# Preparing the second chunk's operands in a hybrid decoder layer: two steps per twelve matmuls, loads one piece ahead

## The chip, the cores and the metric

The kernel runs on one core of a Trainium2 chip. The metric is the device time of one execution in microseconds (us), lower is better. Besides the engines TensorE (PE), VectorE (DVE), ScalarE (ACT) and GpSimd (POOL) there is SyncE (SP), whose queue issues all of this kernel's DMAs. Each engine runs its own instructions in the order in which they stand in its queue; semaphores hold an instruction back until what it needs is there.

## The reference

One decoder layer on 2048 tokens of width 1024 in float32. What matters here is its first part: a norm, and one wide projection `w_in`, whose columns are split into attention inputs, a short gated convolution and two gates.

```
xn = rms_norm(h, mix_norm[l])
proj = jnp.einsum("bsd,dp->bsp", xn, w_in[l]) + b_in[l]
q, k, v, cb, cc, cx, ga, gc = jnp.split(proj, splits, axis=-1)
attn = sliding_window_attention(q, k, v, sinks[l])
conv = cb * causal_depthwise_conv(cc * cx, conv_w[l])
merged = (jax.nn.sigmoid(ga) * jnp.einsum("bsc,cd->bsd", attn, w_attn_branch[l])
          + jax.nn.sigmoid(gc) * jnp.einsum("bsc,cd->bsd", conv, w_conv_branch[l]))
h = h + jnp.einsum("bsd,de->bse", merged, w_out[l])
```

After it come a second norm, an up projection with a convolution and a gate, a down projection and a last norm.

## The kernel before

The tokens are cut into four blocks of 512, and two blocks make a chunk. Float32 products are made of three matmuls each: every operand is held as a high and a low half (`split`, L263: ACT casts the high half, DVE subtracts to get the low one).

The input projection (`project_pairs`) runs once per chunk: a first pass over chunk 0 and a second over chunk 1. It takes the 128-column tiles of the weights in pairs, and computes the two tiles of a pair for the two blocks of a chunk with seven half-size products in place of eight (`strassen`, Strassen-Winograd form). Each of the seven is a call of `mms` with twelve matmuls, and these work on prepared combinations: four weight tiles per pair, called A, S21, S3 and S4, and seven operands of the tokens, x1_0 to x1_6 for the second chunk. The weights of a pair come as two raw loads, `wra` (L194) and `wrb` (L195), and are combined and split on DVE and ACT into `wh` tiles (L264, L265); A comes from `wra` alone. A `wh` tile is fetched three uses ahead.

The first pass has fourteen pairs, numbered 3 to 16: six of the convolution's inputs (3 to 8), then eight of gates (9 to 16). For pair f the order is A (two products), S4 of the pair before (two), S21 (two), S3 (one). Between products ACT copies partial sums out of PSUM: at L818 after A's first product, at L827 after S21's first, at L833 after S3's, at L809 after S4's last. The copy at L827 has one product, the other one of S21, before PE needs its bank again. For gate pairs ACT then computes the sigmoid (L494) and SP stores it (`sgd`, L496). For convolution pairs the function `take` uses two `a` buffers, and the results `cvh`, `cvl` are stored at L516 and L517.

Beside the first pass the second chunk is prepared, by a generator named `fill`. `mms` calls `next(fill)` once after its twelve matmuls, and each call records one step. The steps are: `norm1` for blocks 2 and 3 (two rounds of loads L354 and L363, and a store `xnd` L347), and then `x_operands(1)`. That makes eight pieces, one for each of four row tiles and two halves of 256 tokens. A piece is one run of `operands`: four loads `xb` (L746), a sum on DVE (L749), two more on DVE (L752, L754), four casts `xoh` on ACT and four subtractions `xol` on DVE, and fourteen stores `xopd` (L741, L742) of the seven operands, high and low. It has five steps, the first of which is the loads, and its tiles are all from the pool `e`, which has seven buffers of 128x512 and is also used by S3's weight sums and the convolution's results. The second pass loads the stored operands (L782) as x1.

A scheduler orders the recorded instructions of each engine before the program is built. So the queue's order differs from the order of the code by some rows.

Of the kernel before, what the change touches and what calls it, by code (L numbers as in the profile page):

```python
# [21 lines left out]
F32 = mybir.dt.float32  # L22
# [5 lines left out]
P = 128  # L28
S = 2048
D = 1024  # L30
T = 512
# [65 lines left out]
def layer_kernel(ctx: ExitStack, tc: tile.TileContext, x, w, bcol, g1, g2, gf, cw, fcw, sinks, out):  # L97
# [9 lines left out]
    pool = {"wr": p_wr}  # L107
# [8 lines left out]
    def dram(name, shape, dt=F32):  # L116
        return p_d.tile(shape, dt, name=name, tag=name)
# [7 lines left out]
    xn_d = [[dram(f"xnd{c}_{k}", [P, T]) for k in range(KD)] for c in range(NCH)]  # L125
    xop_d = [[dram(f"xopd{d}_{i}", [P, 2, 4, T]) for i in range(7)] for d in range(2)]
# [18 lines left out]
    state = {"next": 0, "use": 0}  # L145
# [138 lines left out]
    def row_tile(name, tag, bufs=1):  # L284
        return p_rows.tile([P, T], F32, name=name, tag=tag, bufs=bufs)
# [63 lines left out]
    def norm1(c):  # L349

        acc = row_tile(f"acca{c}", "acc")
        for k in range(KD):
            t = tmp(f"xs{c}_{k}")
            nc.sync.dma_start(out=t, in_=x[c, k])  # L354
            square_sum(acc, t, k)
            yield
        rows = {}
        rstd_later(acc, f"a{c}", lambda rb: rows.update(rb=rb))
        while not rows:
            yield  # L360
        for k in range(KD):
            t = tmp(f"xn{c}_{k}")
            nc.sync.dma_start(out=t, in_=x[c, k])  # L363
            scale_x(c, k, t, rows["rb"])
            yield

    def x_operands(d):
        for k in range(4):
            for h in range(2):
                yield from operands(d, k, "x", xn_d, xop_d[d], slice(h * T // 2, (h + 1) * T // 2), "e", "e")  # L370

    def take_k(c, src):
        hi, lo = (tmp(f"k{s}{c}", dt=F32R) for s in "hl")
# [101 lines left out]
    def project_pairs(d, xs, fill, early):  # L475
        ccs, ys = {}, {}

        def begin(f, n, u):
            i = PAIRS[f][n]
            if I_CX <= i < I_GA:  # L480
                if d == 0:
                    nc.gpsimd.memset(u[:, 0:2], 0.0)
                else:
                    nc.scalar.copy(out=u[:, 0:2], in_=uh[:, i - I_CX, :])

        def done(f, g, v):
            for n, t in enumerate((g, v)):
                take(PAIRS[f][n], t, t[:, 2:])

        def take(i, t, whole):  # L490
            halves = [(2 * d + n, whole[:, n * T:(n + 1) * T]) for n in range(2)]
            b = bc[:, i:i + 1]
            if i >= I_GA:
                nc.scalar.activation(out=whole, in_=whole, func=AF.Sigmoid, bias=b)  # L494
                for c, half in halves:
                    nc.sync.dma_start(out=sg_d[c][(i - I_GA) % 8][:, (i - I_GA) // 8, :], in_=half)  # L496
            elif i >= I_CX:
                ct = i - I_CX
                nc.vector.scalar_tensor_tensor(out=whole, in0=whole, scalar=b, in1=ccs.pop(ct), op0=ALU.add, op1=ALU.mult)
                nc.scalar.copy(out=uh[:, ct, :], in_=t[:, 2 * T:])  # L500
                ys[ct] = y = pool["a"].tile([P, 2 * T], F32, name=f"cy{d}_{ct}", tag="a")
                nc.scalar.activation(out=y, in_=whole, func=AF.Copy, scale=cwc[:, ct * 3 + 2:ct * 3 + 3])
                for k in (1, 0):
                    nc.vector.scalar_tensor_tensor(out=y, in0=t[:, k:k + 2 * T], scalar=cwc[:, ct * 3 + k:ct * 3 + k + 1],
                                                   in1=y, op0=ALU.mult, op1=ALU.add)
            elif i >= I_CC:
                ccs[i - I_CC] = cc = pool["a"].tile([P, 2 * T], F32, name=f"cc{d}_{i}", tag="a")
                nc.scalar.activation(out=cc, in_=whole, func=AF.Identity, bias=b)
            elif i >= I_CB:
                ct = i - I_CB  # L510
                y = ys.pop(ct)
                nc.vector.scalar_tensor_tensor(out=y, in0=whole, scalar=b, in1=y, op0=ALU.add, op1=ALU.mult)
                for n, (c, _) in enumerate(halves):
                    hi, lo = (tmp(f"cv{s}{c}_{ct}", dt=F32R) for s in "hl")
                    split(hi, lo, y[:, n * T:(n + 1) * T])
                    nc.sync.dma_start(out=conv_d[c][:, 0, ct, :], in_=hi.bitcast(F32))  # L516
                    nc.sync.dma_start(out=conv_d[c][:, 1, ct, :], in_=lo.bitcast(F32))  # L517
            else:
                for c, half in halves:
                    if i == I_K:  # L520
                        take_k(c, half)
                    elif i == I_V:
                        take_v(c, half)
                    else:
                        take_q(c, i - I_Q, half)

        xs.extend(load_x(xop_d[d], f"x{d}", i) for i in range(len(xs), 5))
        return strassen(d, FIRST[d], xs, lambda: [load_x(xop_d[d], f"x{d}", i) for i in range(len(xs), 7)], begin, done,
                        early, fill)
# [188 lines left out]
    def operands(d, k, name, src, dst, cs, big, split_to, direct={}):  # L718

        n_cs = cs.stop - cs.start

        def get(what, tag, dt=F32):
            return pool[tag].tile([P, 2, n_cs], dt, name=f"{name}{what}{d}_{k}_{cs.start}", tag=tag)

        def out(src, places):

            here = [i for i, place in enumerate(places) if place in direct]  # L730
            for i in here:
                if places[i] < 2:
                    continue
                split(*(direct[places[i]][:, s, k, cs] for s in range(2)), src[:, i, :])
            n = len(here)
            if n == len(places):
                return
            hi, lo = (get(f"o{s}{places[0]}_", split_to, F32R)[:, n:len(places), :] for s in "hl")
            split(hi, lo, src[:, n:, :])
            for i, place in enumerate(places[n:]):  # L740
                nc.sync.dma_start(out=dst[place][:, 0, k, cs], in_=hi[:, i, :].bitcast(F32))  # L741
                nc.sync.dma_start(out=dst[place][:, 1, k, cs], in_=lo[:, i, :].bitcast(F32))  # L742

        b1, b2 = get("b1_", big), get("b2_", big)
        for t, i, n, kk in ((b1, 0, 0, k), (b1, 1, 1, k + 4), (b2, 0, 1, k), (b2, 1, 0, k + 4)):
            nc.sync.dma_start(out=t[:, i, :], in_=src[2 * d + n][kk][:, cs])  # L746
        yield
        t13 = get("t_", big)
        nc.vector.tensor_tensor(out=t13, in0=b1, in1=b2[:, 0:1, :].to_broadcast([P, 2, n_cs]), op=ALU.subtract)  # L749
        out(b2[:, 1:2, :], [1])  # L750
        yield
        nc.vector.scalar_tensor_tensor(out=b2[:, 0, :], in0=b1[:, 1, :], scalar=-1.0, in1=t13[:, 0, :], op0=ALU.mult,  # L752
                                       op1=ALU.subtract)
        nc.vector.scalar_tensor_tensor(out=b2[:, 1, :], in0=b2[:, 0, :], scalar=-1.0, in1=b2[:, 1, :], op0=ALU.mult,  # L754
                                       op1=ALU.subtract)
        out(b1, [0, 5])
        yield
        out(t13, [3, 4])
        yield
        out(b2, [2, 6])  # L760
        yield
# [190 lines left out]
    with ExitStack() as inp:  # L952
        def ipool(name, bufs):
            return inp.enter_context(tc.tile_pool(name=f"{name}i", bufs=bufs))

        pool.update(a=ipool("a", 2), wrf=ipool("wrf", 3), e=ipool("e", 7), u=ipool("u", 3), x7=ipool("x7", 1))
        bc = load_const(bcol, [P, 34], "bc")
        xs = plain()
        g2c = load_const(g2, [P, KD], "g2c")
        gfc = load_const(gf, [P, KD], "gfc")  # L960
        cwc = load_const(cw, [P, 12], "cwc")
        fcwc = load_const(fcw, [P, 3 * 2 * NF], "fcwc")
        sinkb = load_const(sinks.to_broadcast([P, NH]), [P, NH], "sinkb")
        fill = chain(norm1(2), norm1(3), x_operands(1))
        xs = project_pairs(0, xs, fill, lambda: [load_x(xop_d[1], "x1", i) for i in range(2)])
        for _ in fill:
            pass
        early = project_pairs(1, xs, iter(()), lambda: [load_t16(q_d[0], "q0"), load_t16(conv_d[0], "conv0")])
        for what in ("x7", "wrf", "e", "u", "a"):
            del pool[what]  # L970
    with ExitStack() as mix:
# [22 lines left out]
        fill = up_operands(0, "b4", "b4", dict(enumerate(xs)))  # L994
# [79 lines left out]
```

## Time and profile before

| | us |
|---|---|
| median of 3 runs | 2537.17 (2535.75 to 2542.23) |
| profiled execution | 2534.93 |
| its span, first to last instruction | 2533.2 |
| PE busy in the span | 2465.8 |
| first pass of the projection, first to last product in PE's timeline | 78 to 340 |
| loads of pieces (L746), first and last | 211.1 to 313.2 |

The rows shown further on are from one profiled execution. A row of a timeline has the start in us from the span's start, the duration, the engine, the line, the operation, what it writes and reads, and how many were merged; in brackets stands idle time before it and what ended it. SPq is SP's queue of DMA issues: the duration there is that of the issue, not of the transfer. A row of the view of waits says which engine and line waited for which, in us in total, how often, and the longest. A row of the groups has the count, then busy us and the mean in ns, then idle time before it.

### The profile page before, as it was taken

The numbers are of one execution on the slowest core, as the hardware profiler recorded it, in microseconds if no ns is written. First come the engines' busy times: TensorE is split into PE (matmuls) and PEld (weight loads), VectorE is DVE, ScalarE is ACT, GpSimd is POOL, SyncE is SP. The second block draws the span as 40 slices with busy tenths as digits, with TensorE's granted clock in tenths as the row PEclk, the third lists the DMA queues.
The fourth block names the chain that finished last, engine by engine and source line by source line (L and its number), as shares of the span: only waits on it lengthen the run. The fifth ranks groups of instructions, "written<-read, shape, count | busy, mean of one in ns | idle before, by whom it ended". The sixth has DMA issues, their size and how long they took to land.

```text
span 2533.2 us, 30315 instructions
## 1 busy us (share of the span) xinstructions
PE 2465.8 (97%) x11032; PEld 2025.7 (80%) x11032; DVE 1782.6 (70%) x2282; ACT 1119.4 (44%) x1843; POOL 22.6 (1%) x72
## 2 busy tenths in 40 slices
PE   8999999999989898988999999999999999999998
PEld 7888778888868787876888888888888888888886
DVE  8877656664388676776888888755479888875335
ACT  6545444444476353533555555322135555551001
POOL 0000000000000000000000000000000000000000
PEclk9999999999999999999999999999999999999999
DMA  6557895223568869588452333888463333356421
GB/s 197 177 177 238 270 365 174 92 100 112 199 229 283 297 222 322 205 295 313 172 174 101 115 118 100 326 311 304 168 228 116 117 109 100 117 191 256 176 84 67
DMA packets 191221, 488.66 MB, mean 193 GB/s; under 512 B 22112, under 2 KB 41696, under 8 KB 181728
## 3 DMA queue, kind: packets, MB, share of 16 engines
q1 hardware_dynamic: 191072, 486.73, 55.1%
q8 instruction: 86, 1.41, 0.2%
q14 instruction: 63, 0.52, 0.1%
HBM read 325.17 MB, written 161.48 MB: 192 GB/s over the span
## 4 chain that ended last, share of the span: by engine, by line
PE 85%; DMA 6%; DVE 3%; ACT 3%; issue 2%; SPq 2%; POOLq 0%; POOL 0%; DVEq 0%; ACTq 0%
PE upx L795 10%; PE upx L796 10%; PE upx L797 10%; PE dn L248 6%; PE dn L247 6%; PE dn L249 6%; PE upz L797 5%; PE upz L795 5%; PE upz L796 5%; PE upy L797 2%; PE upy L796 2%; PE upy L795 2%; PE wo L247 2%; PE wo L248 2%; PE wo L249 2%
## 5 line engine op out<-in xcount | busy, mean ns | idle before, releaser
L795 PE MATMUL upx<-upx,wh 128*128 128x512 f32 x704 | 277.4, 394 | 5.5 <-ACT u L818 3.9
L796 PE MATMUL upx<-upx,wh 128*128 128x512 f32 x704 | 276.5, 393 | 0.0
L797 PE MATMUL upx<-upx,wh 128*128 128x512 f32 x704 | 276.1, 392 | 0.1
L247 PE MATMUL dn<-act,wh 128*128 128x512 f32 x704 | 274.2, 390 | 0.0
L249 PE MATMUL dn<-act,wh 128*128 128x512 f32 x704 | 274.0, 389 | 0.0
L248 PE MATMUL dn<-act,wh 128*128 128x512 f32 x704 | 273.9, 389 | 0.0
L898 DVE TENSOR_TENSOR hr<-dn,hr 128x512 f32<-128x512 f32 x192 | 131.4, 689 | 198.7 <-PE dn L249 198.6
L856 DVE SCALAR_TENSOR_TENSOR a<-u,fcwc,a 128x1024 f32<-128x1024 f32 x176 | 224.0, 1282 | 50.2 <-ACT a L854 47.5
L264 ACT CAST wh<-ws 128x1024 fp32r<-128x1024 f32 (+1 forms) x150 | 124.8, 834 | 147.5 <-DVE ws L207 68.2
L264 ACT CAST wh<-wr 128x1024 fp32r<-128x1024 f32 (+1 forms) x72 | 69.8, 976 | 258.8 <-PE dn L249 218.8
L795 PE MATMUL upx<-x,wh 128*128 128x512 f32 x440 | 173.1, 393 | 6.6 <-ACT u L827 3.7
L265 DVE TENSOR_TENSOR wh<-ws,wh 128x1024 fp32r<-128x1024 f32 (+1 forms) x150 | 143.1, 955 | 46.7 <-ACT wh L264 46.2
L796 PE MATMUL upx<-x,wh 128*128 128x512 f32 x440 | 172.2, 391 | 0.0
L797 PE MATMUL upx<-x,wh 128*128 128x512 f32 x440 | 172.1, 391 | 0.1
L795 PEld LDWEIGHTS upx<-upx,wh 128*128 128x128 f32 x704 | 132.7, 188 | 36.8 <-ACT u L818 4.3
L797 PEld LDWEIGHTS upx<-upx,wh 128*128 128x128 f32 x704 | 132.7, 189 | 29.9 <-DVE wh L265 0.7
L796 PEld LDWEIGHTS upx<-upx,wh 128*128 128x128 f32 x704 | 132.8, 189 | 28.5
L247 PEld LDWEIGHTS dn<-act,wh 128*128 128x128 f32 x704 | 132.1, 188 | 27.5
L249 PEld LDWEIGHTS dn<-act,wh 128*128 128x128 f32 x704 | 132.1, 188 | 27.5
L248 PEld LDWEIGHTS dn<-act,wh 128*128 128x128 f32 x704 | 132.2, 188 | 27.3
L796 PE MATMUL upz<-upx,wh 128*128 128x512 f32 x352 | 137.1, 389 | 0.8 <-DVE upx L265 0.8
L795 PE MATMUL upz<-upx,wh 128*128 128x512 f32 x352 | 137.1, 389 | 0.0
(274 smaller groups left out, 5385.4 us busy)
## 6 DMA issues: line engine op xcount, KB each, us to landing
act<-actd SPq DMA_DIRECT2D x20, 2048.0 KB, 9.7
wrb<-in_w_dram SPq DMA_DIRECT2D x75, 512.0 KB, 3.7
wra<-in_w_dram SPq DMA_DIRECT2D x75, 512.0 KB, 3.7
wr<-in_w_dram SPq DMA_DIRECT2D x64, 512.0 KB, 5.6
actd<-ach SPq DMA_DIRECT2D x88, 256.0 KB, 2.2
actd<-acl SPq DMA_DIRECT2D x88, 256.0 KB, 2.4
upx<-upd SPq DMA_DIRECT2D x10, 2048.0 KB, 9.4
sgd<-u SPq DMA_DIRECT2D x64, 256.0 KB, 2.9
```

Source lines behind the costliest of these rows:

```text
L247: nc.tensor.matmul(ps, ah, bh, start=start, stop=False)
L248: nc.tensor.matmul(ps, ah, bl, start=False, stop=False)
L249: nc.tensor.matmul(ps, al, bh, start=False, stop=stop)
L264: nc.scalar.copy(out=dh, in_=src)
L265: nc.vector.tensor_sub(out=dl, in0=src, in1=dh.bitcast(F32))
L795: nc.tensor.matmul(bank, ah, bh, start=start and k == 0, stop=False, skip_group_check=True)
L796: nc.tensor.matmul(bank, ah, bl, start=False, stop=False, skip_group_check=True)
L797: nc.tensor.matmul(bank, al, bh, start=False, stop=stop and k == 3, skip_group_check=True)
L856: nc.vector.scalar_tensor_tensor(out=a, in0=u[:, k:k + 2 * T], scalar=w3[k], in1=a, op0=ALU.mult, op1=ALU.add)
L898: nc.vector.tensor_tensor(out=hs[n][j], in0=ps, in1=hs[n][j], op=ALU.add)
```

## The change

Three things are changed. The generator `fill` is wrapped in `twice`, so that a call of `next(fill)` takes two steps. `x_operands` waits with its first piece until the last convolution pair is done (a flag set in `take`), and then records the loads of a piece before the steps of the piece ahead of it. And a piece's four loads go into one tile of the pool `a` (two buffers of 128x1024) in place of two tiles of the pool `e`; its sum `xt` stays in `e`.

```
     def x_operands(d):
-        for k in range(4):
-            for h in range(2):
-                yield from operands(d, k, "x", xn_d, xop_d[d], slice(h * T // 2, (h + 1) * T // 2), "e", "e")
+
+        while not state.get("convolved"):
+            yield
+        parts = [operands(d, k, "x", xn_d, xop_d[d], slice(h * T // 2, (h + 1) * T // 2), "a", "e")
+                 for k in range(4) for h in range(2)]
+        next(parts[0])
+        for n, part in enumerate(parts):
+            if n + 1 < len(parts):
+                next(parts[n + 1])
+            yield from part
+
+    def twice(steps):
+        while True:
+            for _ in range(2):
+                if next(steps, steps) is steps:
+                    return
+            yield
...
+                if ct == 3:
+                    state["convolved"] = True
...
-        b1, b2 = get("b1_", big), get("b2_", big)
+        if big == "a":
+            b = pool["a"].tile([P, 4, n_cs], F32, name=f"{name}b{d}_{k}_{cs.start}", tag="a")
+            b1, b2, big = b[:, :2, :], b[:, 2:, :], split_to
+        else:
+            b1, b2 = get("b1_", big), get("b2_", big)
...
-        fill = chain(norm1(2), norm1(3), x_operands(1))
+        fill = twice(chain(norm1(2), norm1(3), x_operands(1)))
```

The first pass has 98 products. The flag is set after the 44th. Before, the pieces' 40 steps took 40 products; now a piece's four steps after its loads take two products, and the eight pieces sixteen.

The instructions are the same ones, in another order within the first pass; from the second pass on each engine's order is the same as before. The first place is SP's queue, around the raw weights of pair 12 (`wra_12`), the tenth pair of the pass. In the name `xb_1_0_0` the numbers are chunk, row tile and first token of the half; the changed kernel's `xb_0_0` has only the last two. Before, they stood here, right behind the first piece's loads:

```order
L516 DMA convd_141<-cvh_3_1994 128x512
L517 DMA convd_141<-cvl_3_1995 128x512
L363 DMA xn_7_2015<-in_x_dram 128x512
L746 DMA xb_1_0_0_2032<-xnd_0_94 128x256
L746 DMA xb_1_0_0_2032<-xnd_4_106 128x256
L746 DMA xb_1_0_0_2033<-xnd_0_102 128x256
L746 DMA xb_1_0_0_2033<-xnd_4_98 128x256
L347 DMA xnd_7_109<-xn_7_2015 128x512
L741 DMA xopd_1_118<-xoh_1_0_0_2059 128x256
L742 DMA xopd_1_118<-xol_1_0_0_2060 128x256
L741 DMA xopd_0_117<-xoh_1_0_0_2091 128x256
L741 DMA xopd_5_122<-xoh_1_0_0_2091 128x256
```

The next row is `wra_12`. In the changed kernel SP's queue begins the pieces like this (L766 is what was L746, L757 and L758 what were L741 and L742):

```order
L530 DMA convd_140<-cvh_3_1992 128x512
L766 DMA xb_0_0_2019<-xnd_0_94 128x256
L531 DMA convd_140<-cvl_3_1993 128x512
L530 DMA convd_141<-cvh_3_1998 128x512
L531 DMA convd_141<-cvl_3_1999 128x512
L766 DMA xb_0_0_2019<-xnd_4_106 128x256
L766 DMA xb_0_0_2019<-xnd_0_102 128x256
L766 DMA xb_0_0_2019<-xnd_4_98 128x256
```

and comes to the same weights here, behind the stores of the sixth piece (`1_2_256`):

```order
L757 DMA xopd_4_121<-xoh_1_2_256_2435 128x256
L758 DMA xopd_4_121<-xol_1_2_256_2436 128x256
L757 DMA xopd_2_119<-xoh_1_2_256_2443 128x256
L758 DMA xopd_2_119<-xol_1_2_256_2444 128x256
L757 DMA xopd_6_123<-xoh_1_2_256_2443 128x256
L758 DMA xopd_6_123<-xol_1_2_256_2444 128x256
L194 DMA wra_12_2453<-in_w_dram 128x1024
L195 DMA wrb_12_2454<-in_w_dram 128x1024
L766 DMA xb_3_256_2471<-xnd_3_97 128x256
```

From the first `xb` row to `wra_12` it was 9 rows, and now it is 120: 28 loads and 84 stores of pieces, four gate stores, three convolution stores and `wrb_11`. The raw weights of pair 13 follow 38 rows after `wra_12`.

The second place is ACT's queue, from the copy at L827 of pair 11 on. Before:

```order
L827 COPY u_0_11_2252<-upx_11_2249 128x512
L264 CAST xoh_1_1_0_2341<-xb_1_1_0_2292 128x512
L264 CAST xoh_1_1_0_2371<-xt_1_0_2318 128x512
L264 CAST wh_2401<-ws_12_2402 128x1024
L264 CAST xoh_1_1_0_2392<-xb_1_1_0_2293 128x512
L833 ACTIVATE u_0_11_2400<-upx_11_2249 128x512
L818 COPY u_0_12_2430<-upx_12_2427 128x512
```

The cast of `wra_12` stood earlier than these rows. In the changed kernel (L847 is what was L827) it stands among them:

```order
L847 COPY u_0_11_2380<-upx_11_2377 128x512
L264 CAST xoh_1_2_256_2414<-xb_2_256_2317 128x512
L264 CAST xoh_1_2_256_2435<-xt_2_256_2404 128x512
L264 CAST xoh_1_2_256_2443<-xb_2_256_2317 128x512
L264 CAST xoh_1_3_0_2478<-xb_3_0_2399 128x256
L264 CAST xoh_1_3_0_2486<-xb_3_0_2399 128x512
L264 CAST xoh_1_3_0_2507<-xt_3_0_2476 128x512
L264 CAST xoh_1_3_0_2515<-xb_3_0_2399 128x512
L264 CAST wh_2452<-wra_12_2453 128x1024
L264 CAST wh_2530<-wrb_11_2197 128x1024
L264 CAST wh_2593<-ws_12_2594 128x1024
```

Seven casts of the sixth and seventh piece have moved ahead of the cast of `wra_12`.

## The prediction

> **What bounds the kernel now.** I read the page first (spans, busy shares), then who PE waited for in the stretch that the change touches, then the timelines of PE, SP, ACT and DVE around each of those waits. The page's head says that TensorE is the bound:
>
> ```profile
> span 2533.2 us, 30315 instructions
> PE 2465.8 (97%) x11032; PEld 2025.7 (80%) x11032; DVE 1782.6 (70%) x2282; ACT 1119.4 (44%) x1843; POOL 22.6 (1%) x72
> ```
>
> So an edit that leaves the matmuls alone can only move the gaps between them. The view of waits, for PE alone and 60 to 700 us (both passes of the input projection), has all the gaps that the edit can reach:
>
> ```profile
> PE upx L795 <- ACT u L827: 3.7, 3, 2.6
> PE upx L795 <- ACT wh L264: 2.1, 1, 2.1
> PE upx L795 <- ACT u L833: 0.7, 1, 0.7
> ```
>
> That is 6.5 us in all: three waits for the copy at L827, one for a weight cast, one for the copy at L833. In PE's timeline, two of the L827 waits lie late in the first pass:
>
> ```profile
> 266.04 0.39 PE L797 MATMUL upz<-x,wh 128*128 128x512 f32 x1
> 266.86 0.50 PE L795 MATMUL upx<-x,wh 128*128 128x512 f32 x1 [0.43 <-ACT u L827]
> ...
> 304.99 0.39 PE L796 MATMUL upz<-x,wh 128*128 128x512 f32 x1
> 305.22 0.39 PE L797 MATMUL upz<-x,wh 128*128 128x512 f32 x1
> 308.23 0.50 PE L795 MATMUL upx<-x,wh 128*128 128x512 f32 x1 [2.63 <-ACT u L827]
> ```
>
> Matmuls start 0.23 us apart, so twelve (one product) take 2.7 us. Start to start, the gap at 266 costs 0.82 - 0.23 = 0.6 us and the one at 305 costs 3.01 - 0.23 = 2.8 us, 3.4 us together. Both come while the pieces of the second chunk's operands are prepared. ACT and DVE, which run in order, stand in front of a piece whose load is not there yet (waits of ACT and DVE, 200 to 340 us):
>
> ```profile
> ACT xoh L264 <- DMA xb<-xnd: 18.1, 6, 5.4
> DVE xt L749 <- DMA xb<-xnd: 13.8, 7, 3.8
> ```
>
> What they queue behind that is late too, the copy at L827 among it. That is what the change attacks.
>
> **What the change does to those gaps.** A piece's load now stands a whole piece ahead, so the 18.1 and 13.8 us of waiting should go nearly to nothing, and the preparation ends many products before 305 us. I count the 3.4 us as gained. The gap for the weight cast (2.1 us, in the second pass at 376 us, while 2 MB loads of the second chunk fill the DMA engines) stays: orders from there on are the same. The gap at L833 (0.7 us) lies at 170 us, and whether it stays decides nothing here.
>
> **What it costs: SP's queue.** Each of the eight pieces issues four loads and fourteen writes (seven operands, high and low), 18 DMAs, all on SP: 144. SP issues them one at a time. Where it waits for nothing, the timeline of SP shows the rate:
>
> ```profile
> 294.16 0.43 SPq L741 DMA_DIRECT2D xopd<-xoh  x1
> ...
> 297.10 1.90 SPq L746 DMA_DIRECT2D xb<-xnd  x4
> 299.04 0.43 SPq L194 DMA_DIRECT2D wra<-in_w_dram  x1
> ```
>
> From 294.16 to 299.04 are ten issues (six writes, four loads): 0.488 us each. A piece costs SP 18 x 0.488 = 8.8 us. Before, a piece had five products, 13.6 us, so SP kept up. Now it has two products, 5.4 us. Eight pieces want 70 us of SP, and the order has them in 16 products, 44 us. By itself that is harmless: nobody reads these operands before the second pass. It matters for what is queued behind them, and the order of SP shows that: the weights of the tenth pair (wra_12, wrb_12) stand behind seven of the eight pieces' loads and six of their write-backs. From the first load of a piece to wra_12 are 120 issues; before, they were nine.
>
> Is SP early enough? Before, SP did this:
>
> ```profile
> 207.37 0.38 SPq L516 DMA_DIRECT2D convd<-cvh  x1
> ...
> 211.10 2.12 SPq L746 DMA_DIRECT2D xb<-xnd  x4
> ...
> 219.65 0.33 SPq L194 DMA_DIRECT2D wra<-in_w_dram  x1
> ```
>
> The last line is wra_12. PE's first product with it:
>
> ```profile
> 249.69 0.40 PE L797 MATMUL upx<-x,wh 128*128 128x512 f32 x1
> 249.93 0.39 PE L795 MATMUL upx<-xnT,wh 128*128 128x512 f32 x1
> ```
>
> So the weights had a lead of 30 us, of which little was needed: landing, cast and subtraction by the view of this tile are
>
> ```profile
> L264 ACT CAST wh<-wra x75: 1033/1049/1055, 52.0 to 2239.5; 128x1024 fp32r<-128x1024 f32 x75
> L265 DVE TENSOR_TENSOR wh<-wra,wh x75: 1209/1225/1227, 53.1 to 2240.5; 128x1024 fp32r<-128x1024 f32 x75
> ...
> DMA to landing us min/median/max: 3.2/3.7/20.4
> ```
>
> Now for the new time of wra_12. The first load of a piece stands right behind the convolution write of 207.37, the first of the second tile's; nothing ahead of it on SP, ACT or DVE gets later, so it starts at about 207.9. Then 120 x 0.488 = 58.6 us: 266.5. To this come SP's own waits. The first write can't go before its load has landed; in the trace ACT began the first cast here:
>
> ```profile
> 217.09 0.41 ACT L264 CAST xoh<-xb 128x256 fp32r<-128x256 f32 x1 [2.78 <-DMA xb<-xnd]
> ```
>
> 3.9 us after the four loads were issued (211.10 + 2.12). Now six rows of SP, 2.9 us, lie in between, so about 1 us is left. I add another 1 us for a write that waits for DVE behind the weights' subtractions. wra_12 is issued at about 268.5, lands at 272.2, is cast by 273.3. PE wants it at 249.9, since all that it can do before is as long as before: 23.4 us of idle PE. The third matmul needs the low half too, 1.2 us after the cast, 0.5 of which two matmuls cover: 0.7 us more. And after so long an idle time the matmuls may start slowly, as at the kernel's start:
>
> ```profile
> 7.56 0.63 PE L249 MATMUL kv<-xu,wh 128*128 128x512 f32 x1
> 7.99 0.63 PE L247 MATMUL kv<-xu,wh 128*128 128x512 f32 x1
> ...
> 9.69 0.40 PE L248 MATMUL kv<-xu,wh 128*128 128x512 f32 x1
> ```
>
> 0.43 us apart until 9.69, after 6.18 us without a matmul. The seven matmuls from 6.18 to 9.69 took 3.5 us where 1.6 are usual: 1.9 us lost, and I count it once. (The 2.8 us gap at 305 had no such start.)
>
> The rest hides. ACT now has seven fill casts between the copy at L827 and the cast of wra_12: 0.62 us each at most, done long before 272. Where those casts wait for one of the seven "e" buffers, ACT's copies and so PE wait earlier, between 239 and 258 us, but wra_12's time is set by SP, so that is idle time taken earlier and not more of it. The next pair's weights (wra_13) stand 38 issues further on, 18.5 us; a pair has 7 products, 19 us: just in time, with up to 1 us at risk. After that SP has only weights and gates left, with every buffer free, and it catches up within a pair. The norms' two steps per product move 48 DMAs forward in the convolution's pairs; a weight moves there by at most a few rows, with 20 us or more of lead: zero. The "a" buffers are idle until the second pass: zero.
>
> **The sum.** +23.4 (idle for wra_12) +0.7 (its low half) +1.9 (slow restart) -3.4 (gaps at 266 and 305) = +22.6 us. The profiled execution took 2534.93 us (its span and 1.7 us around it): 2557.5. The median of the runs shown is 2.2 us above it, so I forecast 2559.7, say 2559 us.
>
> Bounds of the unknown parts. If an issue cost only 0.42 us (the 0.33 to 0.38 of a lone one and its gap, as from 207.37), the 120 would take 50.4 us, 8.2 less, and without SP's waits and the slow restart it is 12 us less: +10.5, 2548. The other end is SP waiting for casts as often as before (view of waits of SP, 205 to 330 us):
>
> ```profile
> SPq L741 <- ACT xoh L264: 19.4, 9, 3.5
> SPq L742 <- DVE xol L265: 8.0, 14, 1.2
> ```
>
> 27 us over eight pieces, 3.4 each. For six pieces that is 20.5 us where I counted 2: +41, 2578. I stay near the lower value, because most of those waits were ACT's waits for loads, which the change removes.
>
> **Rivals.**
> *The gaps go and nothing comes* (not slower). The loads ahead do what they are for, and SP keeps up. Then 3.4 us go, with the smaller ones at 170 and 227 at most 5.5: 2531.7 to 2533.8. For that wra_12 has to be issued by 249.9 - 1.05 - 3.7 = 245.2, so 120 issues in 37.3 us: 0.31 us each. No row shows such a rate; 0.49 stands in all full stretches. Chance 4%. The Trainium skill, "DMA: Bandwidth & Descriptors", section "Anatomy of one DMA", puts the sequencer's dispatch at some 50 ns and descriptor generation at a small amount; by it, as an estimate, 120 issues would take 6 us and this rival would win. This case's trace has 0.49 us from issue to issue on SP instead; the section speaks of GpSimd's path.
> *DVE is the bound, SP is not.* The groups of DVE's lines from 58 to 340 us, and all engines' busy time from 205 to 330 us (DVE's is the fourth column):
>
> ```profile
> L265 DVE TENSOR_TENSOR xol<-xb,xoh 128x512 fp32r<-128x512 f32 (+1 forms) x24 | 14.3, 596 | 3.8 <-ACT xoh L264 3.7
> L749 DVE TENSOR_TENSOR xt<-xb,xb 128x512 f32<-128x512 f32 x8 | 5.5, 692 | 13.8 <-DMA xb<-xnd 13.8
> L265 DVE TENSOR_TENSOR xol<-xt,xoh 128x512 fp32r<-128x512 f32 x8 | 5.5, 688 | 1.5 <-ACT xoh L264 1.0 <-DMA xopd<-xoh 0.2
> L752 DVE SCALAR_TENSOR_TENSOR xb<-xb,xt 128x256 f32<-128x256 f32 x8 | 3.4, 421 | 0.1
> L754 DVE SCALAR_TENSOR_TENSOR xb<-xb 128x256 f32<-128x256 f32 x8 | 3.4, 421 | 0.1
> ...
> 205.00:330.00 125.00, 121.27 (x529) 98.80 (x528) 87.36 (x131) 67.49 (x98) 0.00 (x0) 1.00 0.82 272
> ```
>
> The pieces are 32 us of DVE's 87; the other 55 are 0.44 us per us. In 44 us DVE would have 32 + 19 = 51 us of work, 7 more than fit. With SP out of the way that is up to 7 us of idle PE, less the 3.4 gained: +3.6, 2541. Chance 5%.
> *The buffers bind instead of SP.* A piece takes nine "e" tiles and there are seven. A tile is free when its last write has landed. If casts and writes wait in turn for each other, a piece costs 11 to 12 us in place of 8.8, six of them 13 to 19 more: 2573 to 2579. It decides where SP shows waits of over 2 us in each piece. For it: DMA engines are 0.82 busy already. Against: a tile stands about 4 us (cast, subtraction, two issues, landing), and seven of them in 8.8 us leave room. Chance 16%.
>
> That leaves 73% for the forecast, and 2% for a gain that I can't name. About 0.3% (7.6 us) is what a measurement of this kernel can tell from no change: 2529.6 to 2544.8. Faster than that would need more than all 6.5 us of PE's waits here: 2%. Within it are the first two rivals: 9%. Slower: 89%. The range of 8 in 10 goes from the low bound, 2548, up into the third rival, 2575.
>
> **What would show it.** Right: in the trace after, one gap of PE of over 10 us ahead of the tenth pair's first product (L795, upx from xnT), released by the cast or the landing of wra; SP issuing without a break for 50 us from about 208; wra of that pair issued 45 to 52 us later than before; the gap at 305 gone; pass two as before. Wrong: wra issued before 246, or PE's largest gap behind a copy at L827 or L833 with SP idle; then the queue was not the cause.

## The result, and the profile after

The changed kernel takes **2561.97 us** (2560.08 to 2563.73, four runs) against 2537.08 us of the kernel before on the same chip: a ratio of 1.0095, with a 95% interval of 1.0081 to 1.011. It is 24.9 us slower. The profiled execution took 2560.08 us (span 2558.3), 25.15 us above the one of before. Lines have moved: the matmuls are L815 to L817 now, the copies once at L827 and L833 are L847 and L853, the pieces' loads L766, their stores L757 and L758.

The view of waits, for PE alone in the two passes of the projection (60 to 720 us), shows where the time is:

```profile
PE upx L815 <- ACT wh L264: 14.1, 2, 12.0
PE upx L815 <- ACT u L853: 10.4, 1, 10.4
PE upx L815 <- ACT u L847: 1.8, 3, 0.7
```

What was 6.5 us is 26.3 us, and nearly all of it is two gaps. In PE's timeline:

```profile
237.72 0.39 PE L817 MATMUL upz<-x,wh 128*128 128x512 f32 x1
248.50 0.79 PE L815 MATMUL upx<-x,wh 128*128 128x512 f32 x1 [10.38 <-ACT u L853]
...
262.13 0.40 PE L817 MATMUL upx<-x,wh 128*128 128x512 f32 x1
274.54 0.79 PE L815 MATMUL upx<-xnT,wh 128*128 128x512 f32 x1 [12.01 <-ACT wh L264]
...
294.33 0.50 PE L815 MATMUL upx<-x,wh 128*128 128x512 f32 x1 [0.68 <-ACT u L847]
```

The first gap waits for pair 10's copy of S3's product (L833 in the old numbers), the second for the cast of `wra_12`: the row at 274.54 is the tenth pair's first product, which was at 249.93. It is 24.6 us late. The old gap at 305 us is gone. The one at 266 us is not: the row at 294.33 is the same matmul, six products behind the tenth pair's first as before, and it waits for the same copy, 0.68 us where it was 0.43. SP's timeline, from the first piece's loads to `wra_12`, and SP's own waits from 205 to 290 us:

```profile
205.40 0.42 SPq L766 DMA_DIRECT2D xb<-xnd  x1
207.45 3.69 SPq L766 DMA_DIRECT2D xb<-xnd  x7
...
268.62 0.45 SPq L194 DMA_DIRECT2D wra<-in_w_dram  x1
```

```profile
SPq L758 <- DVE xol L265: 2.3, 5, 1.1
SPq L757 <- ACT xoh L264: 1.5, 3, 0.9
```

These are SP's largest waits, and all of them together are 10 us of the 85. For the rest SP issues without a break, and the raw weights come out at 268.62 in place of 219.65. ACT is the engine that waits in the same stretch, and not for the pieces' loads any more:

```profile
ACT xoh L264 <- DMA xopd<-xoh: 23.3, 12, 3.5
ACT xoh L264 <- DVE xol L265: 5.7, 6, 1.3
ACT xoh L264 <- DMA xb<-xnd: 1.4, 1, 1.4
```

A cast `xoh` that waits for "DMA xopd" waits for a buffer: the "e" tile that it writes still has a store to land. ACT's timeline at the second gap:

```profile
265.62 0.40 ACT L264 CAST xoh<-xb 128x256 fp32r<-128x256 f32 x1 [2.83 <-DMA xopd<-xoh]
267.63 0.62 ACT L264 CAST xoh<-xb 128x512 fp32r<-128x512 f32 x1 [1.60 <-DMA xopd<-xoh]
269.61 0.62 ACT L264 CAST xoh<-xt 128x512 fp32r<-128x512 f32 x1 [1.36 <-DMA xopd<-xoh]
271.54 0.62 ACT L264 CAST xoh<-xb 128x512 fp32r<-128x512 f32 x1 [1.31 <-DVE xol L265]
273.44 1.04 ACT L264 CAST wh<-wra 128x1024 fp32r<-128x1024 f32 x1 [1.29 <-DMA wra<-in_w_dram]
```

The cast of `wra_12` waited only 1.29 us for its load to land. The casts in front of it, held back by buffers that SP's stores had not freed, ended at 272.2. So two paths lead from SP to this gap, the weights behind 120 issues and the casts behind the stores, and they arrived within 1.3 us of each other.

### The profile page after: what moved, and what is told of

Same layout as the page of the kernel before. It is cut to its first block, busy times and chain, and to the rows that moved or that the text cites. A ratio compares the mean times of both kernels' runs of the same rounds, so it can differ in the third digit from the quotient of the medians.

```text
span 2558.3 us, 30328 instructions
## 1 busy us (share of the span) xinstructions
PE 2468.6 (96%) x11032; PEld 2027.1 (79%) x11032; DVE 1783.7 (70%) x2282; ACT 1121.5 (44%) x1843; POOL 23.3 (1%) x72
## 4 chain that ended last, share of the span: by engine, by line
PE 86%; DMA 5%; DVE 3%; ACT 2%; issue 2%; SPq 2%; POOLq 0%; POOL 0%; DVEq 0%; ACTq 0%
PE upx L815 10%; PE upx L816 10%; PE upx L817 10%; PE dn L249 6%; PE dn L247 6%; PE dn L248 6%; PE upz L815 5%; PE upz L817 5%; PE upz L816 5%; PE upy L816 3%; PE upy L815 3%; PE upy L817 3%; PE wo L247 2%; PE wo L248 2%; PE wo L249 2%
## 5 line engine op out<-in xcount | busy, mean ns | idle before, releaser
L815 PE MATMUL upx<-upx,wh 128*128 128x512 f32 x704 | 276.8, 393 | 5.6 <-ACT u L838 3.9
L817 PE MATMUL upx<-upx,wh 128*128 128x512 f32 x704 | 275.9, 392 | 0.1
L815 PE MATMUL upx<-x,wh 128*128 128x512 f32 x440 | 173.6, 395 | 14.3 <-ACT u L853 10.4
L817 PE MATMUL upx<-x,wh 128*128 128x512 f32 x440 | 172.6, 392 | 0.1
L815 PEld LDWEIGHTS upx<-upx,wh 128*128 128x128 f32 x704 | 132.6, 188 | 36.5 <-ACT u L838 4.3
L817 PEld LDWEIGHTS upx<-upx,wh 128*128 128x128 f32 x704 | 132.6, 188 | 29.8 <-DVE wh L265 0.5
L815 PE MATMUL upz<-upx,wh 128*128 128x512 f32 x352 | 137.1, 389 | 0.0
```

Of the source, the lines that this page charges most:

```text
L815: nc.tensor.matmul(bank, ah, bh, start=start and k == 0, stop=False, skip_group_check=True)
L817: nc.tensor.matmul(bank, al, bh, start=False, stop=stop and k == 3, skip_group_check=True)
```

## The experiments

Each run is compared with the kernel before on the same chip (medians of 2538.5 to 2540 us); the changed kernel stands 24.9 us above before, and differences between experiments are taken between such distances.

**Is it the place of the weights in SP's queue?** The raw weights of the first pass were issued by GpSimd's queue:

```
+            q = nc.gpsimd if where == 0 else nc.sync
-            nc.sync.dma_start(out=r1, in_=w[i1])
-            nc.sync.dma_start(out=r2, in_=w[i2])
+            q.dma_start(out=r1, in_=w[i1])
+            q.dma_start(out=r2, in_=w[i2])
```

> The changed kernel, but the raw weights of the first pass (wra, wrb) are issued on POOL's queue, so that nothing of the pieces stands ahead of them. SP's order of the pieces is the same. ACT's order now has the cast of wra_12 ahead of seven casts of pieces. Theory a (the weights queue behind the pieces on SP): the 12 us gap of PE ahead of pair 12's first product and its slow restart go, the 10.4 us gap behind the copy at L833 stays: 2562 - 12 - 2 = 2548 us. Theory b (SP's rate holds the e tiles, these hold ACT's casts, and these hold ACT's copies, whatever queue the weights are on): the second gap only moves to a copy or another cast on ACT: 2557 to 2562 us. Theory c (DVE has too much work): 2562 us, with DVE busy in the gap.

Measured: 2568.69 us (2565.35 to 2570.53), ratio 1.0116 [1.0101, 1.0131]. `wra_12` was issued at 226.58, 42 us earlier than in the changed kernel, and nothing was won: it is 28.7 us above before. The view of waits of PE, then ACT's timeline in front of the second gap (its L854 is the copy L833 of before):

```profile
PE upx L816 <- ACT u L854: 21.9, 2, 11.5
PE upx L816 <- ACT u L848: 3.5, 3, 1.9
```

```profile
281.65 0.41 ACT L265 CAST xoh<-xb 128x256 fp32r<-128x256 f32 x1 [2.02 <-DMA xopd<-xoh]
283.22 0.62 ACT L265 CAST xoh<-xb 128x512 fp32r<-128x512 f32 x1 [1.16 <-DMA xopd<-xoh]
285.20 0.62 ACT L265 CAST xoh<-xt 128x512 fp32r<-128x512 f32 x1 [1.36 <-DMA xopd<-xoh]
286.57 0.62 ACT L265 CAST xoh<-xb 128x512 fp32r<-128x512 f32 x1 [0.76 <-DVE xol L266]
287.24 0.60 ACT L854 ACTIVATE u<-upx 128x512 f32<-128x512 f32 x1
```

Of the wait for `wra_12`'s cast 0.6 us are left, and a gap as long (11.5 us) stands a pair later, behind the copy of L833, which waits in ACT's queue behind a piece's casts. So the weights' place in SP's queue is not needed for the loss. Why this kernel is some 4 us slower still was not looked into further.

**Is it the rate of SP's issues?** To every low-half store of a piece one more issue was added, of a single row of 1 KB: 56 in all, seven per piece.

```
+                if name == "x":
+                    nc.sync.dma_start(out=dummy_d[0:1, :], in_=lo[0:1, i, :].bitcast(F32))
```

> The changed kernel with 56 more issues on SP, each a store of one row of 1 KB (one partition) behind the store of a low half, to an unused place in DRAM. Compute engines have the same work and the DMA engines nearly so; in contrast to more_issues there are no 4-byte pieces, which made each landing 7 us long. SP has 25 issues per piece in place of 18. Theory of SP's rate: the pieces need 56 x 0.49 = 27 us more of SP, and PE's gaps grow by about as much, less what ends behind the last gap: 2580 us (2574 to 2590). Theory c (DVE has too much work): 2562 us. Theory e (the DMA engines' throughput sets the pieces' pace): 2562 to 2566 us.

Measured: 2593.62 us (2590.15 to 2598.86), ratio 1.0215 [1.0197, 1.0234], a little more than expected. It is 55.2 us above before, 30.3 more than the changed kernel. PE's timeline has three gaps now:

```profile
249.01 0.79 PE L819 MATMUL upx<-x,wh 128*128 128x512 f32 x1 [10.12 <-ACT u L857]
274.86 0.80 PE L819 MATMUL upx<-x,wh 128*128 128x512 f32 x1 [15.66 <-ACT wh L266]
321.83 0.80 PE L819 MATMUL upx<-x,wh 128*128 128x512 f32 x1 [25.08 <-ACT wh L266]
```

The DMA engines had less to do meanwhile, not more (239 GB/s from 205 to 290 us, 276 in the changed kernel), and no work was added to ACT or DVE. But the 30 us can't be booked on SP's issues. The added issues themselves are short: 56 of them, 0.24 us each in the median, 14 us in all. Two waits are new, those of SP and of DVE from 205 to 330 us:

```profile
SPq L762 <- DMA dummyd<-xol: 8.5, 13, 1.4
DVE xol L267 <- DMA dummyd<-xol: 31.1, 11, 4.3
```

All 56 stores write the same row, and 13 times SP (L762) waits for one of them to land before it issues the next. DVE waits for them too: a low half's tile is not free before the store added to it has landed. The run added a chain of stores that hold buffers together with the issues, so it agrees with the expectation in size and does not show that SP's rate is the cause.

An earlier form of this run stored a column, 128 rows of 4 bytes, in place of the one row:

```
+                if name == "x":
+                    nc.sync.dma_start(out=dummy_d[:, i:i + 1], in_=lo[:, i, 0:1].bitcast(F32))
```

> The changed kernel with 56 more issues on SP: one store of 512 bytes to an unused place in DRAM behind each store of a low half. No engine has more work, the bytes are nearly the same. wra_12 stands 156 rows behind the first load of a piece in place of 120. Theory of SP's rate: 36 x 0.49 = 17.6 us more before wra_12: 2579 us (2575 to 2584). Theory c (DVE): 2562 us. Theory d (e tiles): a low tile stands 0.5 to 1 us longer per piece: 2564 to 2568 us.

Measured: 2731.1 us (2728.96 to 2731.85), ratio 1.0756 [1.074, 1.0772], far above all that was expected. Issues from 205 to 290 us, with the median time from issue to landing in the last column:

```profile
xopd<-xoh SPq DMA_DIRECT2D x20, 128.0 KB, 7.2
...
dummyd<-xol SPq DMA_DIRECT2D x19, 0.5 KB, 7.3
```

In the changed kernel the pieces' stores land after 2.1 us. With the 4-byte rows among them all stores land late, so this run says nothing of SP.

**Are the seven "e" buffers short in themselves?** One was taken away:

```
-        pool.update(a=ipool("a", 2), wrf=ipool("wrf", 3), e=ipool("e", 7), u=ipool("u", 3), x7=ipool("x7", 1))
+        pool.update(a=ipool("a", 2), wrf=ipool("wrf", 3), e=ipool("e", 6), u=ipool("u", 3), x7=ipool("x7", 1))
```

> The changed kernel with six e tiles in place of seven. Theory of SP's rate: a piece's nine tiles may stand 8.8 x 6/9 = 5.9 us each, and need 4 to 5 (cast, subtraction, two issues, 2.1 us to land): SP still issues without long breaks, 2562 to 2567 us. Theory d (the e tiles set the pace, SP only follows): a piece takes 7/6 of its time, six pieces 9 to 13 us more: 2572 to 2578 us, with breaks in SP's issues in each piece.

Measured: 2566.87 us (2565.64 to 2569.81), ratio 1.0111 [1.0092, 1.013], 28.4 us above before, 3.5 more than the changed kernel; the two intervals overlap. `wra_12` went out at 272.32, 3.7 us later. With one buffer in seven gone the buffers bind a little at most; their number is not what sets the 25 us.

**What comes next when SP has less to do?** First, the low-half stores were issued by GpSimd's queue, which leaves SP 11 issues per piece:

```
-                nc.sync.dma_start(out=dst[place][:, 1, k, cs], in_=lo[:, i, :].bitcast(F32))
+                (nc.gpsimd if name == "x" else nc.sync).dma_start(out=dst[place][:, 1, k, cs], in_=lo[:, i, :].bitcast(F32))
```

> The changed kernel, but the seven stores of a piece's low halves are issued on POOL's queue: SP has 11 issues per piece, 5.4 us at 0.49, in place of 18. Engines' work, tiles and bytes are the same. Theory of SP's rate (a or b): both long gaps of PE go, 2531 to 2540 us. Theory c (DVE, 7 us more work than fits): about 2541 us, with DVE without idle time from 215 to 255 us. Theory d (seven e tiles for nine per piece): the tiles stand as long or longer, since POOL's issues may be slower: 2555 us or more. If the DMA engines bind (0.83 busy at 274 GB/s; 18.9 MB of pieces in 44 us are 430 GB/s): about 13 us too late, less the lead: 2545 us.

Measured: 2559.43 us (2556.98 to 2561.31), ratio 1.0079 [1.0062, 1.0096], 19.5 us above before and far from what SP's relief should have brought. Busy times from 205 to 290 us (the last two columns are the share of the DMA engines and GB/s), first of the changed kernel, then of this one:

```profile
205.00:290.00 85.00, 61.45 (x248) 48.27 (x247) 54.23 (x88) 38.08 (x61) 0.00 (x0) 0.86 0.83 276
```

```profile
205.00:290.00 85.00, 69.75 (x272) 54.56 (x271) 56.15 (x92) 42.27 (x66) 30.16 (x56) 0.88 0.93 308
```

The DMA engines are 0.93 busy, and the stores land later (issue rows, changed kernel first):

```profile
xopd<-xoh SPq DMA_DIRECT2D x56, 128.0 KB, 2.1
```

```profile
xopd<-xoh SPq DMA_DIRECT2D x56, 128.0 KB, 3.5
xopd<-xol POOLq DMA_DIRECT2D x56, 128.0 KB, 3.6
```

ACT waits nearly as long for buffers as in the changed kernel (20.6 us, ten times, for `xopd<-xol`). PE's gaps are of 2.9, 4.2 and 7.0 us, each with a stretch of slow matmuls behind it. Neither queue is full here: GpSimd's issues take 30 of the 85 us, and SP waits for 26, half of them for casts:

```profile
SPq L757 <- ACT xoh L264: 12.5, 11, 2.5
```

To take GpSimd's queue out of the question, the two stores of one operand tile that go to two places were made one issue of 256 KB, all on SP: 12 issues per piece and the same bytes.

```
+    xop_d = [dram(f"xopd{d}", [7, P, 2, 4, T]) for d in range(2)]
...
+                step = places[-1] - places[0] or 1
+                for s, half in ((0, hi), (1, lo)):
+                    nc.sync.dma_start(out=dst[places[0]:places[-1] + 1:step, :, s, k, cs].rearrange("g p t -> p g t"),
+                                      in_=half.bitcast(F32))
```

> The changed kernel (two steps per product, loads ahead) with the two stores of a tile that go to two operands made one issue of 256 KB: 12 issues per piece on SP in place of 18, all on SP, and the same bytes. If SP's issues alone were the price, 12 x 0.49 = 5.9 us stand against the 5.4 us of two products: wra_12 is issued in time or a few us late, and the time is 2534 to 2545. If the DMA engines are the next bound, as the run with the low-half stores on GpSimd's queue made it look (0.93 busy, landings 3.5 us, 2559), this kernel moves the same bytes at the same pace and shows the same: DMA engines at 0.93 or more between 205 and 290 us, stores landing after 3.5 us or more, casts on ACT waiting for these landings, several gaps of 2 to 8 us, and 2552 to 2564.

Measured: 2557.53 us (2553.95 to 2562.85), ratio 1.0073 [1.0057, 1.009]. Busy times from 205 to 290 us, PE's two long gaps, and SP's row of `wra_12`:

```profile
205.00:290.00 85.00, 67.65 (x276) 53.14 (x275) 56.53 (x91) 43.62 (x66) 0.00 (x0) 0.90 0.95 311
```

```profile
244.93 0.79 PE L821 MATMUL upx<-x,wh 128*128 128x512 f32 x1 [5.48 <-ACT u L859]
...
268.34 0.79 PE L821 MATMUL upx<-xnT,wh 128*128 128x512 f32 x1 [9.44 <-ACT wh L264]
```

```profile
261.50 0.76 SPq L194 DMA_DIRECT2D wra<-in_w_dram  x1
```

With a third of the issues gone, this kernel is still 18.9 us above before. It won 6 us of the 25 (the interval of its ratio just touches that of the changed kernel), at 0.95 of the DMA engines' time. A piece moves 18 x 128 KB, 2.36 MB; at the 308 to 311 GB/s that these two runs reach it needs 7.6 us for itself alone, and two products are 5.4 us. So, by this estimate, the pace of two steps per product does not fit the DMA engines either, whichever queue issues. What the DMA engines cost by themselves is not shown: SP was not out of the way in this run. The two gaps are those of the changed kernel, and `wra_12` still left late, behind 84 issues that took 55.3 us with their waits, 0.66 us each; in the changed kernel it was 120 in 63.2 us, 0.53 us each.

**Two steps per product without the loads ahead.** Only `twice` was put in; `x_operands` is that of before, with five steps per piece (2.5 products) and no wait for the last convolution pair.

```
-        fill = chain(norm1(2), norm1(3), x_operands(1))
+        fill = twice(chain(norm1(2), norm1(3), x_operands(1)))
```

> Two steps per product with the old pieces: loads are a step of their own in the e tiles, no wait for the last convolution pair, so a piece has 2.5 products (6.8 us) and the pieces begin some 60 us earlier. wra_12 stands 151 issues behind the first load of a piece, 74 us, but that first load comes at about 150 us, so wra_12 is issued well before 245 us. If the weights' place in SP's queue were the price, nothing is lost: 2530 to 2540. If SP's rate reaches PE through the e tiles, the casts and the copies of ACT, SP falls behind by 8.8 - 6.8 = 2 us per piece, 16 us in all, of which one or two pieces' buffers absorb a part: 2545 to 2560, with PE's waits named after ACT's copies between 170 and 240 us and none after wra_12's cast.

Measured: 2566.85 us (2562.54 to 2569.35), ratio 1.0105 [1.0088, 1.0122], beyond both ranges. PE's two large gaps, and ACT in front of the longer one:

```profile
216.40 0.79 PE L809 MATMUL upx<-x,wh 128*128 128x512 f32 x1 [8.09 <-ACT wh L264]
256.48 0.79 PE L809 MATMUL upx<-x,wh 128*128 128x512 f32 x1 [18.11 <-ACT wh L264]
```

```profile
251.87 0.92 ACT L264 CAST xoh<-xb 128x256 fp32r<-128x256 f32 x2 [6.91 <-DMA xb<-xnd]
253.83 0.62 ACT L264 CAST xoh<-xt 128x512 fp32r<-128x512 f32 x1 [1.03 <-DVE xol L265]
255.21 0.62 ACT L264 CAST xoh<-xb 128x512 fp32r<-128x512 f32 x1 [0.76 <-DVE xol L265]
255.81 0.62 ACT L264 CAST wh<-ws 128x512 fp32r<-128x512 f32 x1
```

I had expected PE's waits between 170 and 240 us and behind ACT's copies. The first load of a piece came at 164.66, not at about 150, and both gaps stand behind the casts of weight sums instead, at pairs 9 and 10. At the longer one the sum for a weight tile stood behind a piece whose loads had not landed, since SP had issued them late (6.91 us of the waiting). Its ratio and that of the changed kernel overlap: with two steps per product it makes no difference that can be told whether the loads are ahead.

**One step per product, loads ahead.** The reverse: the loads ahead stay, `twice` is left out. A piece then has four steps and four products.

```
-        fill = twice(chain(norm1(2), norm1(3), x_operands(1)))
+        fill = chain(norm1(2), norm1(3), x_operands(1))
```

> The changed kernel without the two steps per product, for norms and pieces alike: the loads one piece ahead in the a tiles stay. A piece has four products, 10.9 us, and SP needs 8.8 us for it. wra_12 stands 17 rows behind the first load of a piece. Theory of SP's rate: no long gap, and the waits for loads of pieces gone: 2531 to 2535 us, a little faster than before. If the two steps were not the cause but the a tiles or the loads ahead: slower than 2545 us. Theory c (DVE): 32 us of pieces over 87 us fit: 2533 to 2537 us.

Measured: 2542.35 us (2540.87 to 2546.48), ratio 1.0015 [1.0006, 1.0024], a little slower than before where a gain was expected. The weights still come late from SP, and ACT waits for them:

```profile
269.87 0.45 SPq L194 DMA_DIRECT2D wra<-in_w_dram  x1
```

```profile
274.76 1.04 ACT L264 CAST wh<-wra 128x1024 fp32r<-128x1024 f32 x1 [3.30 <-DMA wra<-in_w_dram]
```

A piece's 18 issues and its share of gates and weights are some 21.5 issues, 10.5 us of SP; four products are 10.9 us. By this estimate SP only just keeps up, and PE waits 4.8 us in all for two such weight casts in the first pass.

So the loads were made a step of their own, one piece ahead, five products per piece as before:

```
         for n, part in enumerate(parts):
             if n + 1 < len(parts):
                 next(parts[n + 1])
+                yield
             yield from part
...
+        fill = chain(norm1(2), norm1(3), x_operands(1))
```

> The loads one piece ahead in the a tiles alone: one step per product, and the loads of a piece are a step of their own, so a piece has five products (13.6 us) as before the change. SP needs 8.8 us for a piece and 1.7 us for the weights and gates of that time. Theory of SP's rate: it keeps up, the weights are in time, and the waits for the pieces' loads are gone: 3 us faster than before, ratio 0.998 to 1.000. If loads ahead or the a tiles cost something themselves: ratio over 1.002.

Measured: 2537.18 us (2532.25 to 2538.36), ratio 0.999 [0.9981, 1.0], 1.3 us below before: no difference that can be told. Last, the merged stores at one step per product: four products per piece and 12 issues. Beside the lines of the merged kernel above:

```
-        fill = twice(chain(norm1(2), norm1(3), x_operands(1)))
+        fill = chain(norm1(2), norm1(3), x_operands(1))
```

> Loads one piece ahead, one step per product (a piece has four products, 10.9 us), and the two stores of a tile to its two places in DRAM are one issue with the same bytes, 12 issues per piece in place of 18. Theory of SP's rate, with a cost per issue whatever its size: 5.9 + 1.7 = 7.6 us of SP per piece, no late weights: ratio 0.998 to 1.000, where the same pace with 18 issues had 1.0015. If an issue costs by its bytes or rows: as that one, 1.001 to 1.002.

Measured: **2534.89 us** (2531.14 to 2540.04), ratio 0.9984 [0.9975, 0.9993], the fastest of all, 3.6 us below before. Against the one-step kernel only the issues are fewer, 12 per piece in place of 18, at the same pace and with the same bytes, and the two intervals lie apart: this is the pair of runs that shows that SP's issues have a price. In the last two kernels PE has no wait over 0.5 us between 230 us and the one in the second pass. For the merged one, PE's waits in the whole of both passes' stretch:

```profile
PE upx L821 <- ACT wh L264: 2.1, 1, 2.1
PE upx L821 <- ACT u L853: 1.4, 1, 1.4
PE upx L821 <- ACT u L859: 0.7, 1, 0.7
```

## Why the prediction was right, and where not

- **The size and the sign.** 2559 was forecast, with 2548 to 2575 around it; 2561.97 was measured. In the profile the forecast's terms are 24.6 us of idle time (23.4 forecast), 2.6 for the low half and the restart (2.6), -2.5 for the two old gaps (-3.4) and 1.6 in the second pass (0). That is 26.3 us, of which some 1 us is regained in small differences elsewhere.
- **SP's rate and the time of `wra_12`.** The rate was right. That the time is right to 0.1 us, 268.62 against 268.5, is luck, since the terms had errors that cancelled: the first load started 2.5 us earlier than assumed (205.40), and SP's 120 issues and waits took 63.2 us where 60.6 were counted. The load landed in some 4.8 us, not 3.7, and the cast came at 273.44 where it was to be over by 273.3.
- **Idle before the tenth pair.** Counted at 23.4, measured at 24.6 us; the 1.2 us are the landing, nearly all.
- **Idle taken earlier.** As said: 10.4 us of it fell at 238 us, behind pair 10's copy of L833, through casts that wait for buffers.
- **Slow restart.** Counted once, 1.9 us. Ten matmuls from 274.54 to 279.38 took 4.84 us where 2.27 are usual, 2.6 us with the low half's 0.7: right. The earlier gap had a slow stretch too, but that lies within the 24.6 us.
- **The gaps at 266 and 305.** The one at 305 is gone, 2.8 us gained. The one at 266 failed: it stands at 294 now, and start to start it costs 1.06 us where it cost 0.82. So the term is -2.5 us and not -3.4. From the tenth pair's first product to the gap in the second pass it was 123.90 us and is now 123.64: 2.5 gained against 2.6 for the restart, and 0.3 us less in the rest of the way.
- **That the second pass stays as before failed, by 1.6 us.** The gap there has the same 2.50 us from start to start, but the matmuls behind it ran slowly for 3.4 us: they start 0.23 us apart at 401, 0.43 apart from 402.28 to 405.25, and 0.23 apart again from 405.68 on.
- **The cause was put too narrowly.** "wra_12's time is set by SP, so that is idle time taken earlier and not more of it" reads as if the weights' place in the queue were the price. With the weights on another queue the loss stays. What was overlooked is that ACT alone, held at the pace at which SP's stores free the buffers, brings the same delay to whatever stands behind the pieces' casts: a weight cast here, a copy there. What the runs show as the price is the pace: with one step per product, and the loads ahead as in the changed kernel, 2.4 us are left of the loss, and none with five products per piece. How the loss at two products per piece is shared between SP's issues and the DMA engines stays open.
- **The rival "nothing comes"** rested on issues being cheap. The Trainium skill, "DMA: Bandwidth & Descriptors", section "Anatomy of one DMA", gives some 50 ns for a dispatch on GpSimd's path. The changed kernel's trace decides against that as a price for SP's queue: 20 issues from 258.86 to 268.62, 0.49 us each.
- **The rival of the buffers** was to decide where SP waits over 2 us per piece. All SP's waits from 205 to 290 us are 10 us, for eight pieces. Taking a buffer away cost 3.5 us, within the noise; the rival put 13 to 19 on the seven.
- **"DVE is the bound" when SP is out of the way** fell: DVE is busy for 56 to 57 of the 85 us in the two runs with fewer issues on SP. The DMA engines are 0.93 and 0.95 busy there. That they bind in SP's place is argued from this, from the later landings (3.5 us after 2.1) and from the two queues that are not full; no run of its own shows it.

## What to carry to other kernels

Before work beside the matmuls is compressed into fewer of them, its issues are counted against the issue rate of the queue that carries it, and its bytes against the rate of the DMA engines: here 18 issues at 0.49 us and 2.36 MB at 310 GB/s per piece both need more than two products. A full queue delayed not only what stood behind in it; its late stores held buffers, these held an in-order engine, and that held unrelated work which the matmuls needed. The better direction here was fewer issues at one step per product (one issue for a tile that goes to two places), not the same issues faster. A run that is to price one thing has to add that thing alone: the added stores of one row brought waits of their own, and agreed with the forecast all the same.

## What the runs showed of the hardware

- Gaps of the same 2.50 us in the second pass were followed by a slow stretch in the changed kernel, in the last two experiments and in five others, and by none in the kernel before, the one-step kernel and two others. In windows that take in the gap and what follows (PEclk is the third column from the end), first of the kernel before, then of the loads-ahead kernel:

```profile
370.00:385.00 15.00, 12.83 (x56) 9.98 (x55) 7.71 (x11) 4.63 (x7) 0.00 (x0) 1.00 0.89 361
```

```profile
360.00:380.00 20.00, 17.83 (x71) 13.95 (x70) 7.63 (x11) 4.17 (x7) 0.00 (x0) 0.92 0.98 394
```

  The length of the gap alone does not decide it. In the changed kernel it cost 1.6 us; of the 1.3 and 2.2 us by which the last two experiments were ahead at that gap it took back all in one and 1.2 in the other. What does decide was not tried.
- With stores of 128 rows of 4 bytes between them, the pieces' stores landed after some 7 us in place of 2.1, although the DMA engines moved only 112 GB/s.
- GpSimd's queue issues no faster than SP's: 56 issues in 30.16 us, 0.54 us each, where a full stretch of SP has 0.49.
- With the DMA engines 0.95 busy, SP's issues grew longer as well: loads of the same 128 KB took 0.54 us each to issue in the merged kernel and 0.45 in the changed one.
